# Reading the moving operand by two runs in turn in the features, gates, branches, values and up projection

## The chip, the cores and the metric

The kernel runs on one core of a Trainium2 chip (trn2). The metric is the device time of one execution in microseconds. Everything is fp32 data; the matmuls take fp32r operands, and a product is made of three matmuls on split operands (high part and low part).

## The reference, cut to what matters

```python
proj = x @ w_in                      # 256 x 1024 @ 1024 x 3528: q, k, v of three mixers, indexer
o_A  = sparse attention, top-64 keys by an indexer;  o_B = dilated windows;  o_C = causal block
gates  = sigmoid(x @ w_gate)         # 3 gates of 1024 channels
merged = sum_b gates_b * (o_b @ w_br_b)
x = LN(alpha * x + merged @ w_out)
h = square(relu(x @ w_up)) @ w_down  # 1024 -> 4096 -> 1024
x = LN(alpha * x + h + sigmoid(x @ w_ple_gate) * (p @ w_ple))
```

256 tokens, width 1024, one layer.

## The kernel before

A weight arrives by DMA in the tile `raw` (five buffers) and is split by `Weights._split`: ScalarE (ACT) casts it to `whi` (L112, L110), VectorE (DVE) and in part GpSimd (POOL) write the rest `wlo` = raw - whi (L119, L123). `W.get` keeps the splits up to four units ahead of use. `prod` (L189) makes one product: the terms hi*hi, hi*lo and lo*hi, in an order that a table `TURN` gives for each 128-row block. The tables `LOW` and `UP` set at which element of their tiles the 128-column blocks of `whi` and `wlo` lie.

The program goes through these stages, in this order on TensorE (PE):

- **First products** (L501): the four query blocks of the indexer, while x and their weights still arrive.
- **Features, values, gates, branches** (up to about 200 us of the span). The stationary operand (lhsT) is a 128x128 weight block, the moving operand is 256 tokens of `xh` or `xl` (x transposed, 8 blocks of 256 tokens one after the other in a partition), the output a `mm` bank in PSUM. `feat` makes one block of 128 features (24 matmuls of 256 columns), `fill("g")` one block of gates (24), `fill("c")` one block of branches B and C (15, the moving operand is `op`), `merge` two blocks of branch A (18) and then the gated sum. `values` has the tokens stationary and the weights moving, 384 or 328 columns. The attention of 16 heads is strung between: `logits` (L356), softmax on DVE and ACT, transposes (L397), product with V (L401, L402). The gates are the work that PE does while a head waits for DVE and ACT.
- **Out projection, first norm, PLE gate** (about 200 to 245 us): the tokens are stationary, 512 columns of weights move.
- **Up projection** (245 to 336 us): 32 blocks `f`. Each has 8 matmuls of 512 columns (L901, the high and the low part of both token blocks at once) and 8 of 256 (L903). `relu2` (L885 to L887) adds the two parts on DVE and squares on ACT.
- **Down projection, second norm** (336 us to the end): tokens stationary, 512 columns of weights move. Pairs of blocks use Strassen's scheme; `load` and `form` (L854 to L865) bring and combine weights for it, in the tiles `xr`, `rows` and `Y`. The tile of `xr` is the one in which `x1`, the input of the up projection, was.

Three engines read a product out of PSUM: ACT in `q_pair` (L294), `k_pair` (L307) and for the gates (L320), DVE in `q_pair` (L295), `k_pair` (L308), the branches (L335, L336), the merge (L671) and `relu2`. The `mm` banks are three.

The out, PLE and down projections already read their moving operand "by two runs in turn": `wide` takes 512 (or 256) columns as two runs of half the length, of which one element of the first and one of the second are read alternately; `pairs` writes the result side by side, and the host has the weights in such an order (`turns`) that the result comes out in natural order. The runs lie 256 elements, 1 KB, apart. All other matmuls read one run after the other; in the text "plain".

The order of the instructions is set by a scheduler at build time, with some order pinned by hand.

Of the kernel before, what the change touches and what calls it, by code (L numbers as in the profile page):

```python
# [11 lines left out]
F32 = mybir.dt.float32  # L12
F32R = mybir.dt.float32r
ALU = mybir.AluOpType
AF = mybir.ActivationFunctionType
# [6 lines left out]
KT = D // 128  # L22
# [121 lines left out]
def hybrid_layer(ctx: ExitStack, tc: tile.TileContext, x0, xn, pT, wqk, wva, wvb, wg, wbc, wba,  # L144
# [39 lines left out]
    def prod(ps, a, b, first, last, hold=False, more=False, low=2):  # L184

        terms = [(0, 0), (0, 1)]
        terms.insert(low, (1, 0))
        for n, (x, y) in enumerate(terms):
            i = pe.matmul(ps, lhsT=a[x], rhs=b[y], start=first and n == 0, stop=last and n == 2,  # L189
                          skip_group_check=more)  # L190
            if hold and n == 0:
                pin(i)
# [7 lines left out]
    def pairs(ps):  # L200
        return ps.rearrange("p (c a) -> p c a", a=2)

    def gemm(ps, units, xs, k=0):

        for u in units:
            hi, lo = W.get(u)
            for o in range(0, hi.shape[1], 128):
                prod(ps, (hi[:, o:o + 128], lo[:, o:o + 128]), xs[k], k == 0, k == len(xs) - 1,
                     low=TURN["g"][k])
                k += 1  # L210

# [6 lines left out]

    xh = p1.tile([128, KT, S], F32R, name="xh")
    xl = p1.tile([128, KT, S], F32R, name="xl")  # L220
    xs = [(xh[:, k], xl[:, k]) for k in range(KT)]
    n_u = [0]

    def add(*a, at=(0, 0), by=DV):
# [51 lines left out]
    def mmbank(shape):  # L276
        t = mm.tile([128, 512], F32, name="mm", tag="mm")
        return t[:, 0:256] if shape == 256 else t
# [5 lines left out]
    def freed(*ins):  # L284


        if banks_first[0]:
            W.after = tuple(i.ins for i in ins)
        return ins[0].ins

    def q_pair(ps, scale=-0.125):

        q = qpool.tile([128, 2, S], F32R, name="q", tag="q")
        i = (act.mul(q[:, 0], ps, scale),  # L294
             dve.scalar_tensor_tensor(q[:, 1], ps, scale, q[:, 0].bitcast(F32), op0=ALU.mult,  # L295
                                      op1=ALU.subtract))
        freed(*i)
        last[:] = (x.ins for x in i)
        return q

    def k_pair(a, b=None):


        k = (kp if b is None else k1).tile([128, 2, S], F32R, name="k", tag="k")
        for d, ps in ((slice(0, 128), a),) if b is None else ((slice(0, 64), a),
                                                             (slice(64, 128), b)):
            freed(act.copy(k[d, 0], ps),  # L307
                  dve.tensor_tensor(k[d, 1], ps, k[d, 0].bitcast(F32), op=ALU.subtract))  # L308
        return k

    n_g, n_c = [0], [0]
# [1 line left out]
    def fill(what):  # L313


        for w in what:
            if w == "g":
                ps = mmbank(256)
                gemm(ps, u_g[n_g[0]], xs)
                freed(act.activation(G[:, n_g[0]], ps, AF.Tanh, scale=0.5))  # L320
                n_g[0] += 1
                continue
            f = n_c[0]
            n_c[0] += 1
            hi, lo = W.get(u_bc[f][0])
            ps = mmbank(512).rearrange("p (i s) -> p i s", i=2)
            for i, (k0, k1) in enumerate(((3, 5), (5, 8))):
                for k in range(k0, k1):
                    c = slice((k - 3) * 128, (k - 2) * 128)
                    prod(ps[:, i], (hi[:, c], lo[:, c]), (op[:, k, 0], op[:, k, 1]), k == k0,  # L330
                         k == k1 - 1, low=TURN["c"][k - 3])
            g = G[:, 3 * f + 1:3 * f + 3]

            for i, o in ((1, ps[:, 1]), (0, g[:, 0])):
                dve.scalar_tensor_tensor(o, g[:, i], 1.0, ps[:, i], op0=ALU.add, op1=ALU.mult)  # L335
            freed(dve.tensor_tensor(g[:, 0], g[:, 0], ps[:, 1], op=ALU.add))  # L336

    def feat(f):
        ps = mmbank(256)
# [27 lines left out]
    def values(units, n, h0, heads, withiw):  # L367
        pss = [mmbank(512) for _ in range(2)]
        for i in range(4):
            hi, lo = W.get(units[i])  # L370
            for j in range(2):
                k = 2 * i + j
                c = slice(j * n, (j + 1) * n)
                for b in range(2):
                    t = slice(b * 128, (b + 1) * 128)
                    prod(pss[b][:, :n], (xh[:, k, t], xl[:, k, t]), (hi[:, c], lo[:, c]),
                         k == 0, k == KT - 1)
        v_out(pss, n, h0, heads, withiw)

# [97 lines left out]
    with ExitStack() as begin:  # L477
        st = begin.enter_context(tc.tile_pool(name="st", bufs=1, side="right"))
        sh = st.tile([128, KT, FIRST * 128], F32R, name="sh")
        st.tile([128, 32], F32, name="gap")  # L480
        sl = st.tile([128, KT, FIRST * 128], F32R, name="sl")
        st.tile([128, 16], F32, name="pad")
        g0 = G.rearrange("p i s -> p (i s)").rearrange("p (k c) -> p k c", k=KT)
        cut = [((0, 384), (384, 768)) if k == 0 else ((0, 768),) for k in range(KT)]
        with tc.high_priority(offset=1000):
            for k in range(KT):
                for i, (a, b) in enumerate(cut[k]):
                    e = nc.scalar if i else nc.sync
                    e.dma_start(g0[:, k, a:b], x0[k, :, a:b])
            for k in range(KT):  # L490
                act.copy(xh[:, k], g0[:, k, 0:S])
                for a, b in cut[k]:
                    a = max(a, S)
                    act.copy(sh[:, k, a - S:b - S], g0[:, k, a:b])
                dve.tensor_tensor(xl[:, k], g0[:, k, 0:S], xh[:, k].bitcast(F32), op=ALU.subtract)
                dve.tensor_tensor(sl[:, k], g0[:, k, S:], sh[:, k].bitcast(F32), op=ALU.subtract)
        first = [next(ps_s if f < 3 else ps_t)[:, 0:S] for f in range(FIRST)]
        for k in range(KT):
            for i, (w, x) in enumerate(((sh, xh), (sh, xl), (sl, xh))):
                for f in range(FIRST):  # L500
                    pe.matmul(first[f], lhsT=w[:, k, 128 * f:128 * f + 128], rhs=x[:, k],  # L501
                              start=k == i == 0, stop=k == KT - 1 and i == 2)
        iq = [q_pair(ps, 0.125) for ps in first]
    tp, wk, wk2, sm = (right(n, b) for n, b in (("tp", 3), ("wk", 3), ("wk2", 2), ("sm", 6)))
# [156 lines left out]
    def merge(p):  # L661
        hi, lo = W.get(u_ba[p][0])
        ps = mmbank(512).rearrange("p (f s) -> p f s", f=2)
        for f in range(2):
            for k in range(3):
                c = slice((3 * f + k) * 128, (3 * f + k + 1) * 128)
                prod(ps[:, f], (hi[:, c], lo[:, c]), (op[:, k, 0], op[:, k, 1]), k == 0, k == 2,
                     low=TURN["a"][3 * f + k])
        g6 = G[:, 6 * p:6 * p + 6].rearrange("p (f i) s -> p f i s", f=2)
        g = g6[:, :, 0]  # L670
        dve.scalar_tensor_tensor(g, g, 1.0, ps, op0=ALU.add, op1=ALU.mult)  # L671
        dve.tensor_tensor(g, g, g6[:, :, 1], op=ALU.add)
        for f in range(2):
            o = 8192 + 512 * (2 * p + f)
            m = store[:, o:o + 512].rearrange("p (a s) -> p a s", a=2)
            act.mul(m[:, 0], g[:, f], 0.5)
            dve.scalar_tensor_tensor(m[:, 1], g[:, f], 0.5, m[:, 0].bitcast(F32), op0=ALU.mult,
                                     op1=ALU.subtract)
            mt.append(m)
# [202 lines left out]
            u_dn[k] = [add(wdn[k], 1024)]  # L882

    def relu2(dst, ps):
        dve.tensor_reduce(dst, ps.rearrange("p b a t -> p b t a"), axis=AX.X, op=ALU.add)  # L885
        act.activation(dst, dst, AF.Relu)
        act.activation(dst, dst, AF.Square)  # L887

# [2 lines left out]
    for f in range(32):  # L891
        if f == 16:
            with tc.issue_after(W.loads[-1]):
                load(0)
            with tc.issue_after(W.subs[-1]):
                form(0)
        ps = mmbank(512).rearrange("p (b a t) -> p b a t", b=2, a=2)
        hi, lo = W.get(u_up[f][0])
        cs = [slice(k * 128, (k + 1) * 128) for k in range(KT)]
        for k, c in enumerate(cs):  # L900
            pe.matmul(ps, lhsT=hi[:, c], rhs=x1[:, :, k], start=k == 0, stop=False)  # L901
        for k, c in enumerate(cs):
            pe.matmul(ps[:, :, 0], lhsT=lo[:, c], rhs=x1[:, :, k, 0], start=False,  # L903
                      stop=k == KT - 1)
        if f not in half_of:
            spare = f % 2 == 0
            q = (p3.tile([128, 2, 128], F32, name="q1", tag="q1") if spare else
# [166 lines left out]
def _layout(x, p, w_in, w_gate, w_br_a, w_br_b, w_br_c, w_out, ln1_g, ln1_b, w_up, w_down,  # L1074
# [14 lines left out]
    va = np.concatenate([ar(AV, 64), ar(BV, 256), ar(IW, 8)])  # L1089
    vb = ar(CV, 384)  # L1090

    def moving(w, j):
        n = w.shape[1]
        kt = w.shape[0] // 128
        return w.reshape(kt // j, j, 128, n).transpose(0, 2, 1, 3).reshape(kt // j, 128, j * n)

    def turns(w):
        return w.reshape(w.shape[0], 2, 256, 2).transpose(0, 1, 3, 2).reshape(w.shape)

    gate = np.concatenate([ar(b * D + f * 128, 128) for f in range(8) for b in range(3)])  # L1100
    br = np.concatenate([w_br_a[0], w_br_b[0], w_br_c[0]], axis=0)
# [40 lines left out]
```

## Time and profile before

| | |
|---|---|
| median of 3 runs | 425.36 us (424.82 to 425.51) |
| profiled execution | 426.09 us, its span 424.3 us |
| clock granted to TensorE | 0.997 |
| PE, weight loads (PEld), DVE, ACT, POOL busy | 97%, 89%, 83%, 66%, 28% of the span |
| DMA | 84.30 MB, mean 199 GB/s |

A line such as L189 stands for all products, so its groups are told apart by the names of the tiles (`mm<-xh,whi`: written tile, then what is read) and by shape. Matmuls overlap in the pipeline: the duration of one in a row is from its start to its modelled end, and is longer than the distance to the next. The distance, here called the period, is read in the chain of waits, where an unbroken stretch has a length and a count.

### The profile page before, as it was taken

Reading aid. Unit: us, or ns where it says so; the run is one execution under the profiler, and the core shown is the slowest. Engines: PE = TensorE matmul, PEld = TensorE weight load, DVE = VectorE, ACT = ScalarE, POOL = GpSimd, SP = SyncE. Lnnn points to the kernel's source line nnn. Section 1 sums busy time; section 2 is a strip of 40 time slices with the busy share of each in tenths; the row PEclk is TensorE's granted clock in tenths of the full one; section 3 lists DMA queues with packets and bytes.
Section 4 is the critical chain, followed back from the end, with each engine's and each line's share of the span. In section 5 each row is a group of like instructions: output and inputs, shape, how many; then the busy total and the mean of one; then the engine's idle time right before and its main releaser. Section 6 shows DMA issues by size and latency. Waiting matters only on the chain.

```text
span 424.3 us, 7821 instructions
## 1 busy us (share of the span) xinstructions
PE 412.9 (97%) x2804; PEld 378.2 (89%) x2804; DVE 351.7 (83%) x646; ACT 278.7 (66%) x530; POOL 119.1 (28%) x128
## 2 busy tenths in 40 slices
PE   7999999999999999999999999999999999999993
PEld 7989999999999999999887888888888888788883
DVE  4969668977777679879977889989998789899856
ACT  5868366396797785866705568887888756567320
POOL 1568455264353558500000002332320000000001
PEclk9999999999999999999999999999999999999998
DMA  8795976468474407479780686786675177555602
GB/s 291 282 320 157 250 250 204 147 206 273 127 227 137 131 0 269 141 221 336 253 297 13 227 277 199 228 284 173 192 213 182 62 289 242 160 188 188 211 2 100
DMA packets 28300, 84.30 MB, mean 199 GB/s; under 512 B 2992, under 2 KB 7128, under 8 KB 27876
## 3 DMA queue, kind: packets, MB, share of 16 engines
q1 hardware_dynamic: 26880, 79.41, 57.7%
q10 hardware_dynamic: 1284, 4.32, 3.1%
q8 instruction: 22, 0.36, 0.4%
q14 instruction: 18, 0.15, 0.1%
q0 software_dynamic: 96, 0.06, 0.0%
HBM read 81.88 MB, written 1.90 MB: 197 GB/s over the span
## 4 chain that ended last, share of the span: by engine, by line
PE 72%; DVE 10%; DMA 4%; ACT 2%; issue 2%; SPq 0%; DVEq 0%; ACTq 0%
PE mm L189 33%; PE mm L901 14%; PE b L189 13%; PE mm L903 7%; DVE wlo L119 6%; DMA xr<-in_wdn_dram 3%; PE b L356 2%; DMA raw<-in_wdn_dram 1%; PE b L397 1%; ACT whi L112 1%; DVE Y L863 1%; PE b L401 1%; DVE xr L864 1%; DVE rows L863 1%; ACT ri L526 1%
## 5 line engine op out<-in xcount | busy, mean ns | idle before, releaser
L112 ACT CAST whi<-raw 128x1024 fp32r<-128x1024 f32 (+3 forms) x92 | 89.7, 987 | 37.4 <-PE b L189 12.8
L123 DVE TENSOR_TENSOR wlo<-raw,whi 128x256 fp32r<-128x256 f32 (+3 forms) x118 | 96.8, 844 | 16.7 <-ACT whi L112 14.4
L189 PE MATMUL mm<-xh,whi 128*128 128x256 f32 x336 | 90.3, 280 | 0.0
L189 PE MATMUL mm<-xl,whi 128*128 128x256 f32 x336 | 88.1, 279 | 0.0
L123 POOL TENSOR_TENSOR wlo<-raw,whi 128x384 fp32r<-128x384 f32 (+1 forms) x50 | 68.4, 1378 | 70.3 <-ACT whi L112 69.7
L189 PE MATMUL mm<-xh,wlo 128*128 128x256 f32 x336 | 80.8, 282 | 0.3 <-DVE k L308 0.3
L189 PEld LDWEIGHTS mm<-xh,whi 128*128 128x128 f32 x336 | 63.2, 188 | 0.8
L901 PE MATMUL mm<-x,whi 128*128 128x512 f32 x256 | 63.4, 390 | 0.0
L189 PEld LDWEIGHTS mm<-xl,whi 128*128 128x128 f32 x336 | 63.2, 188 | 0.1
L189 PEld LDWEIGHTS mm<-xh,wlo 128*128 128x128 f32 x336 | 58.0, 188 | 0.9 <-DVE k L308 0.5
L189 PE MATMUL b<-whi,store 128*128 128x512 f32 x168 | 52.7, 381 | 0.3 <-DVE b L974 0.3
L901 PEld LDWEIGHTS mm<-x,whi 128*128 128x128 f32 x256 | 45.8, 188 | 7.5
L119 DVE TENSOR_TENSOR wlo<-raw,whi 128x1024 fp32r<-128x1024 f32 (+2 forms) x38 | 43.0, 1154 | 3.0 <-ACT whi L112 3.0
L718 POOL TENSOR_TENSOR rs<-rs,half 128x1 f32<-128x1 f32 x4 | 2.7, 664 | 145.1 <-DVE rs L717 145.1
L110 ACT CAST whi<-raw 128x256 fp32r<-128x256 f32 x64 | 36.7, 617 | 10.0 <-PE mm L901 5.9
L189 PEld LDWEIGHTS b<-whi,store 128*128 128x128 f32 x168 | 31.7, 189 | 5.2 <-DVE b L974 0.7
L903 PEld LDWEIGHTS mm<-x,wlo 128*128 128x128 f32 x256 | 33.8, 188 | 2.5
L903 PE MATMUL mm<-x,wlo 128*128 128x256 f32 x256 | 34.3, 277 | 0.0
L189 PE MATMUL b<-wlo,store 128*128 128x512 f32 x84 | 32.2, 384 | 0.7 <-DVE wlo L119 0.6
L924 POOL TENSOR_TENSOR a<-a 128x128 f32<-128x128 f32 x7 | 6.3, 899 | 60.4 <-ACT a L887 48.9
L189 PE MATMUL mm<-op,whi 128*128 128x256 f32 x128 | 22.5, 280 | 0.0
L189 PE MATMUL b<-whi,x 128*128 128x512 f32 x64 | 19.8, 384 | 0.1
(223 smaller groups left out, 823.3 us busy)
## 6 DMA issues: line engine op xcount, KB each, us to landing
raw<-in_wup_dram SPq DMA_DIRECT2D x32, 512.0 KB
raw<-in_wg_dram SPq DMA_DIRECT2D x24, 512.0 KB
raw<-in_wqk_dram SPq DMA_DIRECT2D x18, 512.0 KB
raw<-in_wdn_dram SPq DMA_DIRECT2D x18, 512.0 KB
raw<-in_wout_dram SPq DMA_DIRECT2D x8, 512.0 KB
raw<-in_wpg_dram SPq DMA_DIRECT2D x8, 512.0 KB
T<-tabd SPq DMA_DIRECT2D x24, 128.0 KB
xr<-in_wdn_dram SPq DMA_DIRECT2D x6, 512.0 KB
```

Of the source, the lines that this page charges most:

```text
L110: i = nc.scalar.copy(blocks(hi, a, b), blocks(r, a, b))
L112: i = nc.scalar.copy(hi, r)
L119: i = e.tensor_tensor(lo[:, x], r[:, x], hi[:, x].bitcast(F32), op=ALU.subtract)
L123: i = e.tensor_tensor(blocks(lo, *x), blocks(r, *x), blocks(hi, *x).bitcast(F32), op=ALU.subtract)
L189: i = pe.matmul(ps, lhsT=a[x], rhs=b[y], start=first and n == 0, stop=last and n == 2, skip_group_check=more)
L356: m = pe.matmul(ss[2 * n + h][:, QC[b]], lhsT=q[d, x, c], rhs=k[d, y, 0:128 * (b + 1)], start=i == 0, stop=i == 2)
L397: pe.transpose(t[:, 128 * i:128 * i + 128], P[:, 128 * i:128 * i + 128], ident)
L401: pe.matmul(v, lhsT=V[:, 0, vh], rhs=pt[:, :, 0:256], start=True, stop=False)
L863: dve.tensor_tensor(t[:, 0:1024], r[:, 512:1536], r[:, 0:1024], op=ALU.subtract)
L901: pe.matmul(ps, lhsT=hi[:, c], rhs=x1[:, :, k], start=k == 0, stop=False)
L903: pe.matmul(ps[:, :, 0], lhsT=lo[:, c], rhs=x1[:, :, k, 0], start=False, stop=k == KT - 1)
L924: pool.tensor_tensor(sums[2], a11, a21, op=ALU.subtract)
```

## The change

It makes the matmuls of L501, of features, gates, branches A, B, C, of the values and of the up projection read their moving operand by two runs in turn. For `xh`, `xl` and `op` the runs are the two halves of 256 tokens, 128 elements (512 B) apart. For the values they are the halves of 384 or 328 weight columns (768 or 656 B), and the host orders these columns for it (`turns` in `moving`), so the result is in natural order. For `x1` in the up projection they are the two token blocks, 2048 elements (8 KB) apart. Every output is written contiguously into its bank as before. Where tokens move, token c and token c+128 now lie side by side in PSUM, and whoever reads the bank (`order`) reads it with a step of two elements; the tile it writes (`halves`) keeps its order. `relu2` reads the two parts 256 elements apart in place of 128, and the tokens with a step of two. The gated product in `merge` becomes two instructions of 256 in place of one of 512. The tables `TURN`, `LOW` and `UP` stay.

```diff
+    def inturn(t):
+        return t.rearrange("p (a c) -> p c a", a=2)
+    def order(ps):
+        return ps.rearrange("p (c a) -> p a c", a=2)
+    def halves(t):
+        return t.rearrange("p (a c) -> p a c", a=2)
...
-                prod(ps, (hi[:, o:o + 128], lo[:, o:o + 128]), xs[k], k == 0, k == len(xs) - 1,
+                prod(pairs(ps), (hi[:, o:o + 128], lo[:, o:o + 128]), xs[k], k == 0, k == len(xs) - 1,
...
-    xs = [(xh[:, k], xl[:, k]) for k in range(KT)]
+    xs = [(inturn(xh[:, k]), inturn(xl[:, k])) for k in range(KT)]
...
-        i = (act.mul(q[:, 0], ps, scale),
-             dve.scalar_tensor_tensor(q[:, 1], ps, scale, q[:, 0].bitcast(F32), op0=ALU.mult,
+        hi, lo, ps = halves(q[:, 0]), halves(q[:, 1]), order(ps)
+        i = (act.mul(hi, ps, scale),
+             dve.scalar_tensor_tensor(lo, ps, scale, hi.bitcast(F32), op0=ALU.mult,
...
-                freed(act.activation(G[:, n_g[0]], ps, AF.Tanh, scale=0.5))
+                freed(act.activation(halves(G[:, n_g[0]]), order(ps), AF.Tanh, scale=0.5))
...
-                    prod(pss[b][:, :n], (xh[:, k, t], xl[:, k, t]), (hi[:, c], lo[:, c]),
+                    prod(pairs(pss[b][:, :n]), (xh[:, k, t], xl[:, k, t]),
+                         (inturn(hi[:, c]), inturn(lo[:, c])),
...
-        dve.scalar_tensor_tensor(g, g, 1.0, ps, op0=ALU.add, op1=ALU.mult)
+        for f in range(2):
+            o = halves(g[:, f])
+            dve.scalar_tensor_tensor(o, o, 1.0, order(ps[:, f]), op0=ALU.add, op1=ALU.mult)
...
-        dve.tensor_reduce(dst, ps.rearrange("p b a t -> p b t a"), axis=AX.X, op=ALU.add)
+        dve.tensor_reduce(dst, ps.rearrange("p a t b -> p b t a"), axis=AX.X, op=ALU.add)
...
-            pe.matmul(ps, lhsT=hi[:, c], rhs=x1[:, :, k], start=k == 0, stop=False)
+            pe.matmul(ps, lhsT=hi[:, c], rhs=x1[:, :, k].rearrange("p b a t -> p a t b"),
+                      start=k == 0, stop=False)
...
-            pe.matmul(ps[:, :, 0], lhsT=lo[:, c], rhs=x1[:, :, k, 0], start=False,
-                      stop=k == KT - 1)
+            pe.matmul(ps[:, 0], lhsT=lo[:, c], rhs=x1[:, :, k, 0].rearrange("p b t -> p t b"),
+                      start=False, stop=k == KT - 1)
```

The same is done with `k_pair`, the branches in `fill` and `merge`, and L501.

On no engine does an instruction change its place; what differs is shapes, and the pairs in `merge`. On DVE, where the merges end and the out projection is about to begin (L671 is the gated product, L672 the sum, L677 the low part of the merged features that the out projection loads as weights), the rows before are:

```order
L671 SCALAR_TENSOR_TENSOR G<-G,mm 128x2x256
L336 TENSOR_TENSOR G<-G,mm 128x256
L119 TENSOR_TENSOR wlo<-raw,whi 128x1024
L672 TENSOR_TENSOR G<-G 128x2x256
L671 SCALAR_TENSOR_TENSOR G<-G,mm 128x2x256
L119 TENSOR_TENSOR wlo<-raw,whi 128x1024
L671 SCALAR_TENSOR_TENSOR G<-G,mm 128x2x256
L677 SCALAR_TENSOR_TENSOR store<-G,store 128x256
```

In the changed kernel, where L688, L689 and L694 are the same three lines, the same place on DVE reads:

```order
L688 SCALAR_TENSOR_TENSOR G<-G,mm 128x256 x2
L348 TENSOR_TENSOR G<-G,mm 128x256
L119 TENSOR_TENSOR wlo<-raw,whi 128x1024
L689 TENSOR_TENSOR G<-G 128x2x256
L688 SCALAR_TENSOR_TENSOR G<-G,mm 128x256 x2
L119 TENSOR_TENSOR wlo<-raw,whi 128x1024
L688 SCALAR_TENSOR_TENSOR G<-G,mm 128x256 x2
L694 SCALAR_TENSOR_TENSOR store<-G,store 128x256
```

Three instructions more stand ahead of the first low part that the out projection needs, and nothing else moved.

More of the change, by code (lines that the diff above doesn't have):

```diff
@@ L306, in k_pair @@
                                                              (slice(64, 128), b)):
-            freed(act.copy(k[d, 0], ps),
-                  dve.tensor_tensor(k[d, 1], ps, k[d, 0].bitcast(F32), op=ALU.subtract))
+            hi, lo, ps = halves(k[d, 0]), halves(k[d, 1]), order(ps)
+            freed(act.copy(hi, ps), dve.tensor_tensor(lo, ps, hi.bitcast(F32), op=ALU.subtract))
         return k
@@ L329, in fill @@
                     c = slice((k - 3) * 128, (k - 2) * 128)
-                    prod(ps[:, i], (hi[:, c], lo[:, c]), (op[:, k, 0], op[:, k, 1]), k == k0,
+                    prod(pairs(ps[:, i]), (hi[:, c], lo[:, c]),
+                         (inturn(op[:, k, 0]), inturn(op[:, k, 1])), k == k0,
                          k == k1 - 1, low=TURN["c"][k - 3])
             g = G[:, 3 * f + 1:3 * f + 3]
-            for i, o in ((1, ps[:, 1]), (0, g[:, 0])):
-                dve.scalar_tensor_tensor(o, g[:, i], 1.0, ps[:, i], op0=ALU.add, op1=ALU.mult)
-            freed(dve.tensor_tensor(g[:, 0], g[:, 0], ps[:, 1], op=ALU.add))
+            g, ps = ([halves(g[:, i]) for i in range(2)], [order(ps[:, i]) for i in range(2)])
+            for i, o in ((1, ps[1]), (0, g[0])):
+                dve.scalar_tensor_tensor(o, g[i], 1.0, ps[i], op0=ALU.add, op1=ALU.mult)
+            freed(dve.tensor_tensor(g[0], g[0], ps[1], op=ALU.add))
     def feat(f):
@@ L500, in hybrid_layer @@
                 for f in range(FIRST):
-                    pe.matmul(first[f], lhsT=w[:, k, 128 * f:128 * f + 128], rhs=x[:, k],
+                    pe.matmul(pairs(first[f]), lhsT=w[:, k, 128 * f:128 * f + 128],
+                              rhs=inturn(x[:, k]),
                               start=k == i == 0, stop=k == KT - 1 and i == 2)
@@ L666, in merge @@
                 c = slice((3 * f + k) * 128, (3 * f + k + 1) * 128)
-                prod(ps[:, f], (hi[:, c], lo[:, c]), (op[:, k, 0], op[:, k, 1]), k == 0, k == 2,
+                prod(pairs(ps[:, f]), (hi[:, c], lo[:, c]),
+                     (inturn(op[:, k, 0]), inturn(op[:, k, 1])), k == 0, k == 2,
                      low=TURN["a"][3 * f + k])
@@ L896, in hybrid_layer @@
                 form(0)
-        ps = mmbank(512).rearrange("p (b a t) -> p b a t", b=2, a=2)
+        ps = mmbank(512).rearrange("p (a t b) -> p a t b", a=2, b=2)
         hi, lo = W.get(u_up[f][0])
@@ L1090, in _layout, with turns @@
     vb = ar(CV, 384)
+    def turns(w, n=512):
+        m = len(w)
+        return w.reshape(m, -1, n // 2, 2).transpose(0, 1, 3, 2).reshape(m, -1)
     def moving(w, j):
         n = w.shape[1]
+        w = turns(w, n)
         kt = w.shape[0] // 128
         return w.reshape(kt // j, j, 128, n).transpose(0, 2, 1, 3).reshape(kt // j, 128, j * n)
-    def turns(w):
-        return w.reshape(w.shape[0], 2, 256, 2).transpose(0, 1, 3, 2).reshape(w.shape)
     gate = np.concatenate([ar(b * D + f * 128, 128) for f in range(8) for b in range(3)])
```

## The prediction

> **What bounds the kernel now.** I read the engines' busy times first, then the 20 us stretches, the chain of waits, and the groups with their shapes kept apart. The busy times, and four of the stretches (columns: PE, PEld, DVE, ACT, POOL busy, granted clock, share of DMA, GB/s):
>
> ```profile
> PE 412.9 (97%) x2804; PEld 378.2 (89%) x2804; DVE 351.7 (83%) x646; ACT 278.7 (66%) x530; POOL 119.1 (28%) x128
> ...
> 100.00:120.00 20.00, 20.00 (x180) 19.29 (x179) 15.62 (x43) 15.96 (x34) 9.80 (x7) 1.00 0.57 177
> 180.00:200.00 20.00, 20.00 (x173) 19.90 (x172) 17.58 (x32) 12.95 (x21) 0.74 (x1) 1.00 0.85 276
> 300.00:320.00 20.00, 20.00 (x121) 17.74 (x120) 19.56 (x30) 17.08 (x37) 5.77 (x8) 1.00 0.66 204
> 380.00:400.00 20.00, 19.64 (x91) 16.59 (x90) 19.96 (x23) 11.77 (x13) 0.00 (x0) 1.00 0.60 206
> ```
>
> PE is the bound up to the end of the up projection, at full clock. DVE is close behind it at 300 us and has taken over at 380 us. So what counts for the change is the period of PE's matmuls, and whether DVE lets PE go faster. The periods stand in the chain of waits (start, length, what): plain matmuls of 256 columns (features and gates, at the end branches) in the first three rows, then the 512s and the 256s of one block of the up projection, then 512s and 256s of the down projection, which are already read by two runs in turn.
>
> ```profile
> 40.24 7.58 PE mm L189 x64
> 105.90 7.50 PE mm L189 x64
> 184.93 14.70 PE mm L189 x129
> ...
> 262.51 1.81 PE mm L901 x8
> 264.33 0.91 PE mm L903 x8
> ...
> 408.58 5.18 PE b L189 x24
> 413.76 3.58 PE mm L189 x32
> ```
>
> Length by count is the period: 118, 117 and 114 ns for the plain 256s (a missing record inflates the first two); I take 115. An up block has 226 ns per 512 and 114 per 256. In turn it is 215.8 ns per 512 (5.18/24) and 111.9 per 256 (3.58/32). A second witness is the mean duration, kept apart by shape:
>
> ```profile
> L189 PE MATMUL mm<-xh,whi 128*128 128x256 f32 x336 | 90.3, 280 | 0.0
> L189 PE MATMUL mm<-xl,whi 128*128 128x256 f32 x336 | 88.1, 279 | 0.0
> L901 PE MATMUL mm<-x,whi 128*128 128x512 f32 x256 | 63.4, 390 | 0.0
> L903 PE MATMUL mm<-x,wlo 128*128 128x256 f32 x256 | 34.3, 277 | 0.0
> L189 PE MATMUL mm<-op,whi 128*128 128x256 f32 x128 | 22.5, 280 | 0.0
> L189 PE MATMUL mm<-op,wlo 128*128 128x256 f32 x64 | 15.3, 279 | 0.3 <-DVE wlo L123 0.3
> L189 PE MATMUL mm<-whi,xh 128*128 128x384 f32 x16 | 5.4, 335 | 0.0
> L189 PE MATMUL mm<-whi,xh 128*128 128x328 f32 x16 | 5.1, 320 | 0.0
> L189 PE MATMUL b<-whi,PL 128*128 128x512 f32 x8 | 2.7, 380 | 0.0
> L189 PE MATMUL mm<-whi,store 128*128 128x256 f32 x16 | 3.1, 275 | 0.0
> ```
>
> In turn (last two rows) a 512 is 10 ns shorter and a 256 2 to 5 ns shorter than plain.
>
> **What the change costs and brings, step by step.**
>
> *Features and gates*: 42 blocks of 24 matmuls, 1008 (three groups of 336), 115 - 111.9 = 3.1 ns each: 3.1 us. Ends: 2.1 ns (by the row at 184.93) gives 2.1 us, 5 ns (by the durations) 5.0 us. *Branches*: 128 + 64 = 192 at 2 ns: 0.4 us. *Values*: a 384 in turn should last, between 275 and 380, 328 ns, so 7 ns less, and a 328 305, so 15 less; 48 of each (one row of three terms shown): 1.1 us. *Up*: 256 x (226 - 215.8) = 2.6 us and 256 x (114 - 111.9) = 0.5 us. *L501* waits for x to arrive; nothing. Sum on PE: 7.7 us.
>
> [...]
>
> *PSUM read with a step of two*. No row has step two. The nearest reads stand here, DVE first: the up projection's reduction takes its 512 values with a step of 128, a plain sum takes 512 in order.
>
> ```profile
> L885 DVE TENSOR_REDUCE a<-mm 128x256 f32<-128x512 f32 x23 | 15.6, 684 | 2.8 <-PE mm L903 2.7
> L974 DVE TENSOR_TENSOR b<-b,Y 128x512 f32<-128x512 f32 x2 | 1.4, 690 | 0.0
> L671 DVE SCALAR_TENSOR_TENSOR G<-G,mm 128x512 f32<-128x512 f32 x4 | 2.7, 681 | 0.0
> L335 DVE SCALAR_TENSOR_TENSOR mm<-G,mm 128x256 f32<-128x256 f32 x8 | 3.3, 416 | 0.0
> L320 ACT ACTIVATE G<-mm 128x256 f32<-128x256 f32 x24 | 9.1, 380 | 3.7 <-PE mm L189 3.5
> L774 ACT ACTIVATE PL<-mm 128x512 f32<-128x512 f32 x4 | 2.4, 597 | 11.8 <-PE mm L189 11.8
> ```
>
> DVE pays nothing for a step (684 against 690), so nothing for step two. For ACT there is no stepped PSUM read; the lower end is 0, the upper one a doubled streaming time, which is 597 - 380 = 217 ns per 256 values. I take 0, by DVE's rows, and keep 217 ns x about 49 reads (24 gates, 16 q, 9 k) = 10.6 us of ACT time as a rival.
>
> *Merge*: one 512 becomes two 256s, 2 x 416 - 681 = 151 ns, four times, three of them ahead of the first low part that the out projection loads. That place is tight. DVE's last pause before it ends at 189.24, DVE writes that part at 199.03, and PE loads it as weights at 199.68:
>
> ```profile
> 189.24 0.96 DVE L123 TENSOR_TENSOR wlo<-raw,whi 128x768 fp32r<-128x768 f32 x1 [1.19 <-ACT whi L112]
> ...
> 199.03 0.42 DVE L677 SCALAR_TENSOR_TENSOR store<-G,store 128x256 fp32r<-128x256 f32 x1
> ...
> 199.68 0.19 PEld L189 LDWEIGHTS b<-whi,store 128*128 128x128 f32 x1
> ```
>
> 0.23 us to spare. Without a pause in front of it the part comes 0.45 us later, while PE comes some 0.2 us sooner (about 100 matmuls of 114 ns in that stretch, 2 ns each). PE waits 0.45 + 0.2 - 0.23, some 0.4 us; with what DVE's next parts add I charge 0.5.
>
> *Heads*. PE's order is fixed; between a head's logits and its transposes stand some 10 us of gate matmuls, and they shrink by 2.7%, so 0.3 us, while the softmax on DVE and ACT doesn't. Where nothing is to spare, that comes back as a wait. Two such places, ACT's last scaling and the first transpose that needs it:
>
> ```profile
> 91.43 0.79 ACT L417 ACTIVATE eb<-eb,r 128x128 f32<-128x128 f32 x2
> ...
> 92.30 0.27 PE L397 MATMUL b<-ident,eb 128*128 128x128 f32 x1
> ...
> 112.79 0.80 ACT L417 ACTIVATE e<-e,r 128x128 f32<-128x128 f32 x2
> ...
> 113.24 0.33 PE L397 MATMUL b<-ident,e 128*128 128x128 f32 x1
> ```
>
> Less than 0.1 us to spare in both. I found about eight places among the 16 heads under 0.5 us; at 0.15 us each the loss is 1.2 us. Ends: 0 and 2.4 (all eight, in full).
>
> *Up*: DVE is busy 19.56 of 20 us in the stretch at 300, so a block's 2.72 us (1.81 + 0.91) holds 2.66 of DVE's work, and PE alone would take 8 x 215.8 + 8 x 111.9 = 2.62. PE had no idle time there, so the splits are ahead of it and can lend some; I charge 0.2.
>
> *Down* starts with transfers into the tile that the up projection has just read out, and then runs through DVE:
>
> ```profile
> 335.05 0.92 PE mm L903 x8
> 336.37 0.43 SPq L856
> 336.83 4.83 DMA xr<-in_wdn_dram
> ```
>
> It moves forward as a whole by what is gained before it and gets no shorter.
>
> Sum: 7.7 - 0.5 - 1.2 - 0.2 = 5.8 us. The profiled execution takes 426.09 us (its span of 424.3 and 1.8 around it), which leaves 420.3; it stands 0.7 above the median of 425.36, so I predict 419.5 for the median.
>
> **Rivals.**
>
> *Reading in turn loses at the new distances.* Every row in turn has its runs 1 KB apart; here they are 512 B, 656, 768 B and 8 KB apart. The weight blocks stay where the tables put them. If a 256 at 512 B goes to the 118 ns of the worst plain stretch, 3 ns x 1200 = 3.6 us are lost in front in place of 3.5 gained; with the up projection's 3.1 and the losses of 1.9 that is 425.4 + 3.6 - 1.1 - 3.1 + 1.9, about 427. It decides from about 2 ns per 256 on, if the up projection still gains (3.1 + 1.1 - 1.9 = 2.3 us over 1200). If 8 KB fails as well, it is 430. For it: no row has these distances. Against: two stationary tiles (`PL`, `store`) and two lengths gain alike. Chance 0.14. [...]
>
> *The 256s stay at 114 to 115.* Two loads of weights and a matmul may simply not go faster; in-turn 256s come from 32 matmuls alone. Then features, gates, branches and 256s of the up projection bring nothing, 3.7 us with the values and the 512s remain, and the losses fall to about 0.9: 422.6. Chance 0.11.
>
> *DVE holds the up projection.* If DVE's 2.66 us is the block's time, 32 x 0.04 = 1.3 us are lost, at worst all of 3.1: 421 to 422.5. Against it: DVE's splits were never late (PE has no idle time there). Chance 0.10.
>
> *ACT pays for step two.* Each head's q, and each gate between, is 0.2 us later in ACT's queue, so the eight tight places lose 0.4 more each: 419.5 + 3.2 = 422.7. Chance 0.08. [...]
>
> *Nothing to measure*: two of these together, 424.6 to 425.4. Chance 0.07.
>
> **How the numbers follow.** 0.50 for the forecast (own range 417 to 422), 0.11, 0.10 and 0.08 for the three that leave part of the gain, 0.07 for no change, 0.14 for the slower one. What a measurement here can tell from no change is 0.2%, 0.85 us. Faster 0.79, same 0.07, slower 0.14. The low end is the durations' 5 ns in front (419.5 - 1.9 - 1.2 without head losses = 416.4); the high end, 424.5, takes in the partial gains.
>
> **What would show it.** In the changed kernel's chain, unbroken 256s of gates at about 112 ns and eight 512s of the up projection in 1.73 us in place of 1.81; the gates' ACTIVATE still near 380 and the reduction near 684 ns; a wait of half a microsecond of PE at the start of the out projection; small new waits at L397, L401 or L356; from the first xr transfer to the end 87.5 us as before (424.3 - 336.8). The prediction is wrong if the 256s come out above 115 ns, if ACT's reads near 600, or if the down projection grows by what was gained before it.

## The result, and the profile after

The changed kernel takes 420.25 us (median of 4 runs, 419.57 to 420.44), the kernel before beside it 425.44 (424.82 to 425.86): a ratio of 0.9876, with a 95% interval of 0.9859 to 0.9894. The profiled execution took 420.38 us, its span is 418.6 us.

The busy times, and two of the stretches (PE, PEld, DVE, ACT, POOL busy, granted clock, share of DMA, GB/s):

```profile
PE 405.4 (97%) x2804; PEld 373.6 (89%) x2804; DVE 350.7 (84%) x650; ACT 277.4 (66%) x530; POOL 120.5 (29%) x128
...
180.00:200.00 20.00, 20.00 (x166) 19.56 (x165) 18.00 (x33) 12.61 (x19) 0.00 (x0) 1.00 0.81 280
300.00:320.00 20.00, 20.00 (x125) 18.39 (x124) 19.76 (x33) 17.95 (x40) 5.39 (x7) 1.00 0.70 204
```

The granted clock is full in both kernels (0.997 and 0.996), so a shorter period is not a faster clock. PE's busy time fell by 412.9 - 405.4 = 7.5 us, the span by 5.7: PE now idles 13.2 us in place of 11.4. These 1.8 us are what the waits have to account for.

The chain of waits (start, length, what), with an unbroken row of gates and one block of the up projection:

```profile
45.38 9.20 DMA raw<-in_wqk_dram
...
104.70 7.34 PE mm L189 x64
...
125.16 3.57 PE mm L189 x32
...
185.24 8.70 DMA raw<-in_wout_dram
...
262.55 1.73 PE mm L918 x8
...
264.27 0.89 PE mm L921 x8
...
331.55 4.58 DMA xr<-in_wdn_dram
```

3.57/32 is 111.6 ns for a 256, 1.73/8 is 216 for a 512, 0.89/8 is 111 for the up projection's 256s. Ahead of the down projection the chain of before has no transfer; this one has four, x at 1.65, gate weights at 39.81 and the two shown. PE hardly stops for them (the waits below), so they tell what now ends its waits, not how much time is lost. Of the one at 185.24, out weights, there is more below. By shape (busy us, mean ns):

```profile
L189 PE MATMUL mm<-xh,whi 128*128 128x256 f32 x336 | 89.2, 278 | 0.0
L918 PE MATMUL mm<-x,whi 128*128 128x512 f32 x256 | 60.7, 379 | 0.0
L921 PE MATMUL mm<-x,wlo 128*128 128x256 f32 x256 | 33.7, 275 | 0.0
L902 DVE TENSOR_REDUCE a<-mm 128x256 f32<-128x512 f32 x23 | 15.6, 680 | 0.6 <-PE mm L921 0.3
L330 ACT ACTIVATE G<-mm 128x256 f32<-128x256 f32 x24 | 9.1, 380 | 2.7 <-PE mm L189 2.5
L189 PE MATMUL mm<-whi,xh 128*128 128x384 f32 x16 | 5.2, 326 | 0.0
L189 PE MATMUL mm<-whi,xh 128*128 128x328 f32 x16 | 4.9, 309 | 0.0
```

The matmuls are shorter by 2 to 11 ns than in the prediction's rows. PSUM with a step of two costs ACT nothing (L330, 380 ns before and after) and DVE nothing (L902, 680 against 684). PE's waits, summed by who ended them (us, times, longest), first of the kernel before, then of the changed one:

```profile
PE b L501 <- ACT sh L494: 1.0, 1, 1.0
...
PE mm L189 <- DVE k L308: 0.3, 1, 0.3
```

```profile
PE mm L189 <- DVE k L318: 0.8, 1, 0.8
PE b L514 <- ACT sh L507: 0.7, 1, 0.7
PE b L189 <- DVE store L694: 0.7, 1, 0.7
...
PE mm L189 <- DVE V L399: 0.6, 1, 0.6
```

L318 (L308 before), L399 and L694 are 0.5, 0.6 and 0.7 us of new waiting; L501, now L514, gives 0.2 back (0.75 us after 0.96).

### The profile page after: what moved, and what is told of

It reads as the page before. It is cut to its first block, busy times and chain, and to the rows that moved or that the text cites. A ratio compares the mean times of both kernels' runs of the same rounds, so it can differ in the third digit from the quotient of the medians.

```text
span 418.6 us, 7824 instructions
## 1 busy us (share of the span) xinstructions
PE 405.4 (97%) x2804; PEld 373.6 (89%) x2804; DVE 350.7 (84%) x650; ACT 277.4 (66%) x530; POOL 120.5 (29%) x128
## 4 chain that ended last, share of the span: by engine, by line
PE 66%; DVE 15%; DMA 10%; issue 4%; ACT 2%; POOL 1%; SPq 1%; DVEq 0%; ACTq 0%; POOLq 0%
PE mm L189 26%; PE mm L918 13%; PE b L189 12%; PE mm L921 7%; DVE wlo L119 6%; PE b L368 2%; DMA xr<-in_wdn_dram 2%; DMA raw<-in_wqk_dram 2%; DMA raw<-in_wout_dram 2%; PE b L514 2%; DVE wlo L123 2%; DMA G<-in_x_dram 1%; ACT whi L112 1%; PE b L410 1%; DMA raw<-in_wg_dram 1%
## 5 line engine op out<-in xcount | busy, mean ns | idle before, releaser
L189 PE MATMUL mm<-xh,whi 128*128 128x256 f32 x336 | 89.2, 278 | 0.0
L189 PE MATMUL mm<-xl,whi 128*128 128x256 f32 x336 | 86.9, 276 | 0.0
L189 PE MATMUL mm<-xh,wlo 128*128 128x256 f32 x336 | 79.9, 279 | 1.3 <-DVE k L318 0.8
L189 PEld LDWEIGHTS mm<-xh,whi 128*128 128x128 f32 x336 | 64.4, 192 | 0.9
L189 PEld LDWEIGHTS mm<-xl,whi 128*128 128x128 f32 x336 | 64.5, 192 | 0.1
L918 PE MATMUL mm<-x,whi 128*128 128x512 f32 x256 | 60.7, 379 | 0.0
L942 POOL TENSOR_TENSOR a<-a 128x128 f32<-128x128 f32 x7 | 7.3, 1044 | 58.4 <-ACT a L904 52.8
```

Source lines behind the costliest of these rows:

```text
L918: pe.matmul(ps, lhsT=hi[:, c], rhs=x1[:, :, k].rearrange("p b a t -> p a t b"), start=k == 0, stop=False)
L942: pool.tensor_tensor(sums[2], a11, a21, op=ALU.subtract)
```

## Experiments

*1 and 2: each half of the change alone.* The up projection's edits on the kernel before:

```diff
-        dve.tensor_reduce(dst, ps.rearrange("p b a t -> p b t a"), axis=AX.X, op=ALU.add)
+        dve.tensor_reduce(dst, ps.rearrange("p a t b -> p b t a"), axis=AX.X, op=ALU.add)
...
-            pe.matmul(ps, lhsT=hi[:, c], rhs=x1[:, :, k], start=k == 0, stop=False)
+            pe.matmul(ps, lhsT=hi[:, c], rhs=x1[:, :, k].rearrange("p b a t -> p a t b"),
+                      start=k == 0, stop=False)
```

(and the 256s alike), and the changed kernel with these taken back.

> Only the up projection reads in turn (and its reduction reads PSUM with the new steps); everything ahead of it is the kernel before. Theory (each part's own matmuls give its gain, the parts add up, the rest moves as a whole): 512s of the up projection at 216 ns, its 256s at 111.5, gates stay at 114.5; the up projection 3.2 us shorter than the kernel before, all else unchanged, 425.4 - 3.2 = 422.2 us. Rival (DVE holds the up projection, and the whole change only got its full gain there because PE came sooner): up projection shorter by 2 us or less, total above 423.2.

> Features, gates, branches, values and first products read in turn, the up projection reads plain as before. Theory: 256s at 111.6 ns in place of 114.5, values 9 to 11 ns shorter, some 4.4 us of PE time less up to the out projection, of which about 2.4 us come back as waits (bank releases behind DVE's splits, one head or two, one low part at the out projection); the up projection starts 2.0 us sooner than in the kernel before and 423.4 us in all. Rival (the waits come from elsewhere, so the front's gain is smaller or larger than 2.0): below 422.6 or above 424.4.

All ratios here are to the kernel before. Up alone: 422.38 us, ratio 0.9925 [0.9901, 0.9949]. Front alone: 423.60, ratio 0.9959 [0.9944, 0.9974]. 3.1 and 1.9 us by the medians, together 5.0 beside the 5.2 of both. In the chain of up alone the gates are plain and the up blocks short; in front alone it is the other way round:

```profile
106.06 7.50 PE mm L189 x64
...
293.66 1.73 PE mm L901 x8
```

```profile
104.57 7.34 PE mm L189 x64
...
294.07 1.81 PE mm L918 x8
```

With up alone, DVE is at 19.77 us of 20 in the stretch at 300 and PE at 20.00, so PE's whole gain there arrives. The theory holds for both.

*3 and 4: where the weights lie.* The tables `LOW`, `UP` and `TURN` taken out of the kernel before and of the changed one: every weight block stands right behind the one before, and all blocks use one order of terms.

```diff
-    UP = (16, *range(192, 1088, 128)), (64, *range(208, 1104, 128))
+    UP = (0, 0)
...
-            u.append([add(w[len(u)], n, at=(40, LOW[t]) if t in LOW else (0, 0),
+            u.append([add(w[len(u)], n, at=(0, 0),
...
-    TURN = {"g": (0, 2, 1, 2, 2, 0, 1, 2), "c": (2, 0, 2, 1, 2), "a": (2, 1, 2, 2, 2, 0)}
+    TURN = {"g": (2,) * 8, "c": (2,) * 5, "a": (2,) * 6}
```

> The kernel before with the tables made flat: every block of weights lies right behind the one before it, from element 0 of its tile, and the three terms come in one order throughout. Theory (plain reads meet the weight load that runs beside them, and how often depends on where the weights lie): periods of plain 256s rise from 114.5 to 116 to 120, of the 512s of the up projection from 227 to 228 to 233; 2 to 7 us slower than the kernel before, 427 to 432 us. Rival (places don't matter, plain is slow by itself): 114.5 and 227 stay, 425.4 less up to 1 us since a split in the up projection is one instruction in place of two.

> The changed kernel with the same flat tables. Theory (in turn, moving read and weight load fall into step, so the place of the weights doesn't matter): 111.6 and 216 ns stay, total within 1 us of the changed kernel, 419.3 to 420.5. Rival (in turn depends on places as plain does, the tables happen to fit): 256s above 114, 512s above 220, total 423 or more.

The kernel before becomes slower: 431.01 us, ratio 1.0131 [1.0107, 1.0155]. The changed kernel does not: 419.60, 0.9874 [0.9842, 0.9906]. Chains, the plain one first:

```profile
106.40 7.76 PE mm L189 x64
...
273.60 1.84 PE mm L901 x8
275.44 0.95 PE mm L903 x8
```

```profile
105.25 7.34 PE mm L189 x64
```

Plain, the up block goes from 1.81 + 0.91 us to 1.84 + 0.95; between the starts of neighbouring matmuls in the trace a plain 256 in front takes 118.2 ns in the mean in place of 114.5. In turn it is 111.6 and 216.1, as with the tables. So plain reads depend here on where the weights lie (in the up projection on that alone, since `TURN` does not act there; in front on the places or the order of terms, which were changed together), and reads in turn do not. The theory's periods are borne out; its cause, plain reads that meet the weight load beside them and reads in turn that fall into step with it, is my guess, and no run here shows it.

*5 to 8: what "in turn" has to be.* The tokens by four runs of 64; the gates' tokens by two runs but two neighbours of each at a time; the gates' tokens by two runs only 64 values apart, within each half; the up projection's 512s by four runs of 128.

```diff
+    def many(t):
+        return t.rearrange("p (a c) -> p c a", a=4)
...
+    def by_twos(t):
+        return t.rearrange("p (a c e) -> p c a e", a=2, e=2)
...
+    def near(t):
+        return t.rearrange("p (b a c) -> p b c a", b=2, a=2)
...
-            pe.matmul(ps, lhsT=hi[:, c], rhs=x1[:, :, k].rearrange("p b a t -> p a t b"),
+            pe.matmul(ps, lhsT=hi[:, c], rhs=x1[:, :, k].rearrange("p b a t -> p t a b"),
```

The first three are in the first three kernels, in the place of `inturn`; the last line is the fourth kernel's.

> The changed kernel, but where tokens move (features, gates, branches, first products) 256 tokens are read by four runs of 64 in turn, and PSUM is read with a step of four; values and up projection stay at two runs. Theory (with two runs each run is read at the pace at which the weight load reads its block, so that the two, once in step, don't meet again; with four runs the pace is half of that and they meet now and then): 256s of gates at 112.5 to 118, spread over several ns, total 1 to 5 us above the changed kernel, 421 to 425. Rival (any order in which neighbours in time aren't neighbours in memory does): 111.6 with no spread, 420.2 as the changed kernel. In both the gates' ACTIVATE stays at 380 ns if a step in PSUM costs ACT nothing.

> The changed kernel, but the gates read two neighbouring tokens of the first run, then two of the second, and so on, so every 8 bytes of PSUM are again read together; everything else stays. Theory (pace): the average pace of each run is as with one token at a time, so 111.6 ns, at most 112.5, total 420.2. Rival (what helps is that no two accesses in a row lie side by side): 113 to 114.5 for the 576 matmuls of the gates, features stay at 111.6, total up to 1.6 us above, 421.8.

> The changed kernel, but the gates alone read the tokens by two runs that lie 64 values (256 B) apart, in turn within each half of 128, in place of 128 values (512 B) apart; features stay as they are. ACT puts the values back. Theory one (the number of runs in turn is what counts: two are good at any distance seen): gates stay at 111.6 ns per 256, the time near 420. Theory two (256 B apart is too near, which made the kernel with four runs of 64 slow, 140 ns): gates at 130 to 150 ns, 432 to 445 us.

> The changed kernel, but the up projection's 512s read four runs of 128 in turn, all of them 512 B or more apart, in place of two; their 256s read two runs as before, and write every second place of PSUM. Theory one (number of runs): 512s longer by as much per value as with four runs of 64 tokens (140 against 111.6 per 256), so about 270 ns in place of 216, 256 x 54 ns = 13.8 us more, about 434 us, less what DVE hides. Theory two (distance): 512s at 216 ns, the time near 420.

Four runs of tokens: 451.84 us, 1.0625 [1.0595, 1.0654]. Two neighbours at a time: 449.24, 1.0564 [1.0537, 1.0591]. Two runs 256 B apart: 419.72 (one run), nothing lost. Up by four: 437.24 (one run). What was expected of the first two, by theory and by rival, was far off: neither had expected a 256 above 118 ns, so both are refuted as they stood. Starts of neighbouring matmuls of the timeline, four runs of tokens and then two neighbours at a time:

```profile
119.74 0.30 PE L189 MATMUL mm<-xh,whi 128*128 128x256 f32 x1
...
120.30 0.31 PE L189 MATMUL mm<-xl,whi 128*128 128x256 f32 x1
```

```profile
115.73 0.33 PE L189 MATMUL mm<-xl,whi 128*128 128x256 f32 x1
...
116.91 0.34 PE L189 MATMUL mm<-xh,wlo 128*128 128x256 f32 x1
```

Four steps in 0.56 us are 140 ns, seven in 1.18 us 169 ns, against 111.6. The chains of the other two, 256 B apart and up by four:

```profile
104.75 7.34 PE mm L189 x64
```

```profile
252.03 0.89 PE mm L921 x8
252.92 2.26 PE mm L918 x8
```

Two runs are good at 256 B as at the other distances (7.34 us, as in the changed kernel's stretch at 104.70). Four runs are bad at 64 values as at 512 B and more: 2.26/8 = 282 ns per 512 is 0.55 ns per value, and 140/256 is 0.55 too. So with one value at a time the number of runs decides here, not the distance; theory one of the last two kernels holds (up by four came to 437 where 434 was expected). Why four runs, or pairs out of two, lose is open.

Whether neighbours in memory are read one right after the other does not order them either: of the reads that never do so, those by two runs are the fastest (111.6) and those by four are slow (140); plain reads, which always do, take 114.5 to 118.2, and the reads that take two neighbours at a time are the slowest (169).

ACT's read of the gates with a step of four took 381 ns in the four-run kernel, so for ACT this step costs nothing either (380 with a step of two and in order):

```profile
L336 ACT ACTIVATE G<-mm 128x256 f32<-128x256 f32 x24 | 9.1, 381 | 16.2 <-PE mm L189 16.1
```

*9 and 10: the wait at the out projection.* First without the extra instructions in the merge: branch A is left plain, so that one 512 reads the bank again. Then the changed kernel with the load of X (1 MB), which ACT issues at 185.57 in the midst of the loads of out weights, put on SyncE behind the last of them.

```diff
-        for f in range(2):
-            o = halves(g[:, f])
-            dve.scalar_tensor_tensor(o, o, 1.0, order(ps[:, f]), op0=ALU.add, op1=ALU.mult)
+        dve.scalar_tensor_tensor(g, g, 1.0, ps, op0=ALU.add, op1=ALU.mult)
```

```diff
-    act.dma_start(X, xn)
+    with tc.issue_after(W.loads[-1]):
+        nc.sync.dma_start(X, xn)
```

> The changed kernel, but branch A in merge reads plain, so the gated product is one instruction of 512 again. Theory one (the wait for a low part at the out projection comes from the three or four instructions more on DVE ahead of it): the wait of 0.7 us on the low parts falls to 0.3 or less, total 0.2 to 0.4 us below the changed kernel. Theory two (it comes from the out weights, whose transfers don't land sooner just because PE is there sooner, so ACT casts and DVE splits them late and the low part stands in DVE's queue behind three of them): ACT still waits about 2 us or more for the transfer of out weights at 191 us, the wait on the low part stays at 0.5 to 1.7, total within 0.3 us of the changed kernel.

> The changed kernel, but the transfer of x in rows (1 MB, for the first norm) is issued on SyncE behind the last transfer of out weights, not on ACT's queue in the middle of them. Theory two of the wait (transfers of out weights are what is late): they land sooner by about the 3 to 4 us that 1 MB takes at 280 GB/s, ACT's wait for them at 191 us of 2.1 goes to 0.5 or less, PE's wait on the low part to 0.2 or less, total 0.5 to 0.9 us below the changed kernel, 419.5. Theory one (the merge's extra instructions): PE's wait stays at 0.5 or more, total as the changed kernel, 420.2.

Merge plain: 420.97 us, 0.9890 [0.9847, 0.9933]; X later: 419.70, 0.9866 [0.9843, 0.9888]. The totals do not tell them apart. PE's wait for the low part, of merge plain and of X later:

```profile
PE b L189 <- DVE store L691: 1.4, 1, 1.4
```

```profile
PE b L189 <- DVE store L694: 0.4, 1, 0.4
```

In these traces the wait goes with how long ACT sits before its cast of out weights. That row in the changed kernel, with the tables flat, with X later, and, from the experiments above, with up by four:

```profile
194.03 1.06 ACT L112 CAST whi<-raw 128x1024 fp32r<-128x1024 f32 x1 [2.10 <-DMA raw<-in_wout_dram]
```

```profile
195.87 1.06 ACT L112 CAST whi<-raw 128x1024 fp32r<-128x1024 f32 x1 [3.89 <-DMA raw<-in_wout_dram]
```

```profile
192.55 1.05 ACT L112 CAST whi<-raw 128x1024 fp32r<-128x1024 f32 x1 [0.92 <-PE mm L189]
```

```profile
193.01 1.05 ACT L112 CAST whi<-raw 128x1024 fp32r<-128x1024 f32 x1 [0.92 <-PE mm L189]
```

ACT waits 2.10 and 3.89 us in the first two, where the transfer lands late, and 0.92 in the others, where it waits for PE. PE's wait for L694 is 0.7, 1.6, 0.4 and 0.4 us. Up by four leaves the load of X where it was, and so do near runs, with 0.92 and 0.4 too; front alone has 3.19 and 1.6, merge plain 3.02 and 1.4. (The profiled executions of merge plain and of flat tables, 422.38 and 422.28 us, are the longest of their four.) So there are two parts: 0.4 us that stay when no transfer is late, and up to 1.2 that differ from trace to trace.

*The late transfer.* From issue to landing this load of 512 KB takes 4.2 us in both kernels with X later (the other is number 11). With X beside it, it takes 6.9 in near runs and in up by four, 8.7 in the changed kernel, and 9.7 to 10.4 in front alone, flat tables and merge plain. So theory two is supported as to the transfer: the load of X holds it up; at 6.9 us it is still in time, at 8.7 ACT waits for it. Open is why it takes 3.6 to 4.1 us in the three kernels whose front is plain (before, up alone, the first with flat tables), where X is issued 0.5 us behind it; with the front in turn it is issued 0.3 us behind.

*The 0.4 that stay.* DVE's rows from one split to the third low part, first of the kernel before, then of up by four:

```profile
192.56 1.22 DVE L119 TENSOR_TENSOR wlo<-raw,whi 128x1024 fp32r<-128x1024 f32 x1
...
202.63 3.49 DVE L119 TENSOR_TENSOR store<-raw,store 128x1024 fp32r<-128x1024 f32 x3
206.04 0.76 DVE L677 SCALAR_TENSOR_TENSOR store<-G,store 128x256 fp32r<-128x256 f32 x2
```

```profile
190.10 1.22 DVE L119 TENSOR_TENSOR wlo<-raw,whi 128x1024 fp32r<-128x1024 f32 x1
...
203.84 0.75 DVE L694 SCALAR_TENSOR_TENSOR store<-G,store 128x256 fp32r<-128x256 f32 x2
```

DVE has no pause in either. From the first row to the last it takes 13.48 us before and 13.74 with the pairs: 0.26 more, which is what the four pairs of L688 cost. It reaches the split 2.46 us sooner than before, PE the out projection 2.63 us sooner (196.83 for 199.46): another 0.17. Together that is 0.43, the wait; theory two had expected 0.2 or less with X later. So the extra instructions are a part of it, and theory one is not refuted; merge plain saves them, but its trace has a late transfer, and no run shows it without one.

*11: both ideas together.* Flat tables and X later, on the changed kernel.

> The changed kernel with weight blocks contiguous and one order of terms (the tables LOW, UP and TURN flat), and the load of X issued by SyncE behind the last load of out weights. Each alone ran as fast as the changed kernel within its interval (0.9874 and 0.9866 of the kernel before, against 0.9876). Theory: 256s at 111.6, 512s at 216.1, PE's wait for the first low parts of the out projection at most 0.4 us; 419.5 us, between 418.9 and 420.5. Rival: without the tables the late weights come back as a wait of 1.6 us, 421.

419.87 us, 0.9885 [0.9867, 0.9903]: the wait for L694 is 0.4 and the periods stay, so the late weights of the rival do not come, but the time is that of the changed kernel within the intervals. No version tried here beats it. What the run shows is that the tables can go at no measurable cost: ACT's instructions fall from 530 to 498 and DVE's from 650 to 618.

## Why the prediction was right, and where it was not

Forecast for the profiled execution 420.3 us, measured 420.38; for the median 419.5, measured 420.25, inside the range. The 0.7 us that I took off for the median belonged to the one profiled execution of before; the changed kernel's stands only 0.13 above its median.

**Gain on PE.** Said 7.7, measured 7.5. By the starts of neighbouring matmuls: 1008 x (114.5 - 111.65) = 2.9 for features and gates (said 3.1), 192 x (113.9 - 111.6) = 0.4 for the branches (0.4), 48 x 9 and 48 x 11 ns by the durations = 1.0 for the values (1.1; 7 and 15 ns had been said, two errors that cancel), 256 x (226.8 - 216.2) = 2.7 and 256 x (113.4 - 111.3) = 0.5 for up (2.6 and 0.5). The periods of 24 and 32 matmuls elsewhere in the program carried over to 1712 others. Matched one by one in the two traces, PE's steps are 7.9 us shorter, leaving the waits aside.

**Step two.** Taken as nothing for DVE and for ACT; both measured (680 against 684 ns, 380 against 380). DVE's rows were a fair neighbour for ACT, for which there was none.

**Merge: the sum near, its parts not.** The loss was said to be 0.5 us, and 0.74 came. *Place:* the row at 199.68 that I took for the load of the first low part belongs to a high part. The wait came later, at the third block. DVE stands there behind three splits of out weights, in both kernels (at 202.63 before, at 200.60 now):

```profile
199.34 0.74 DVE L688 SCALAR_TENSOR_TENSOR G<-G,mm 128x256 f32<-128x256 f32 x2
200.00 0.69 DVE L689 TENSOR_TENSOR G<-G 128x512 f32<-128x512 f32 x1
200.60 3.49 DVE L119 TENSOR_TENSOR store<-raw,store 128x1024 fp32r<-128x1024 f32 x3
204.01 0.75 DVE L694 SCALAR_TENSOR_TENSOR store<-G,store 128x256 fp32r<-128x256 f32 x2
...
204.48 1.35 PE L189 MATMUL b<-whi,store 128*128 128x512 f32 x5 [0.74 <-DVE store L694]
```

The first matmul of the out projection starts at 199.46 before and at 196.67 after, 2.79 us sooner; the low part at 206.04 and 204.01, 2.03 sooner. The difference, 0.76, is the wait of 0.74. Nothing was to spare there: the matmul that needs this low part already starts 0.36 us after its neighbour before, in place of 0.22. *Size:* two 256s were charged 2 x 416 - 681 = 151 ns; but DVE's instructions overlap here (the pair runs to 200.08, the next starts at 200.00), and from the pair's start to the next start it is 200.00 - 199.34 = 0.66 us, against 0.59 for the single 512 of before (201.44 to 202.03): 0.07. Four pairs ahead of the third block are 0.26 us, where 0.45 was charged for three; PE comes 0.17 sooner, 0.2 said. *Left out:* the other 0.33, from 13.74 us on DVE to 204.01 - 189.94 = 14.07, is the late transfer: it is issued 2.5 us sooner than before (185.24 for 187.73) and lands 2.1 us later (193.93 for 191.83). The prediction asked what DVE had to spare and not what its data waited for, though its row for 180 to 200 us has a DMA share of 0.85.

**Heads.** 1.2 us said for eight tight places. Matmul by matmul, PE stands longer at three heads, by 0.3, 0.2 and 0.1 us, some 0.6 in all; one is the second place named (113.24 before), where the transpose now starts 0.30 us after the matmul ahead of it; before it was 0.12:

```profile
111.77 0.28 PE L189 MATMUL mm<-xh,whi 128*128 128x256 f32 x1
112.07 0.33 PE L410 MATMUL b<-ident,e 128*128 128x128 f32 x1
```

At the first (92.30) no wait appears. Such waits also differ between traces: up alone, whose front is that of the kernel before, has one of 0.48 us at a head (L401) where the kernel before has none. So one trace does not settle this term.

**Banks, a term that the sum had not.** What I had not looked for is the release of `mm` banks: PE stops where DVE, behind a split, is late to read a bank.

```profile
37.70 1.64 DVE L123 TENSOR_TENSOR wlo<-raw,whi 128x640 fp32r<-128x640 f32 x1
39.26 0.41 DVE L318 TENSOR_TENSOR k<-mm,k 128x256 fp32r<-128x256 f32 x1
...
39.82 0.35 PE L189 MATMUL mm<-xh,wlo 128*128 128x256 f32 x1 [0.77 <-DVE k L318]
```

This one was 0.3 us already and became 0.8, the one at V (L399) is new with 0.6. Both stand in every trace of a kernel whose front reads by two runs throughout, with 0.5 to 0.9 and 0.6 us.

**The sum of the losses.** By the starts of PE's matmuls, banks cost 1.2 us more than before, heads 0.6, the out projection 0.8, a late `wlo` ahead of the branches 0.1; the first products give 0.1 back and the down projection 0.4. That is 2.2, and 7.9 - 2.2 is the 5.7 by which the span fell. (PE's idle time grew by 1.8 only, because the modelled end of a matmul covers the first part of a wait: a 256 lasts 278 ns in its row, at a period of 111.6.) Said were 1.9. That these are so near is in part luck: heads came to half of what was charged and up to nothing, and banks, which were not in the sum, filled the place.

**Up.** 0.2 was charged for DVE, nothing was lost: the stage went from 91.6 us (the chain's end at 335.97) to 88.3, 3.25 less, which is PE's whole gain there. DVE at 19.76 of 20 us still kept ahead. **Down** moved as a whole, but for the 0.4 us: 418.6 - 331.55 = 87.05 us from the first transfer of xr to the end, 87.5 said. That transfer itself took 4.58 us in place of 4.83.

**Rivals.** That other distances lose (0.14) is refuted at 512 B and 8 KB by the result and at 256 B by the gates with near runs; that ACT pays (0.08) by L330; that DVE holds up (0.10) by the run of up alone; that the 256s stay (0.11) by the chain; that there is nothing to measure (0.07) by the result.

## What to carry to other kernels

Where PE is busy all the time, read the period from an unbroken row of the chain of waits (length by count) rather than from the duration of one matmul, and compare it with the period of the same shape elsewhere in the program: it carried over here to within 0.4 ns. Then charge the loss to whatever does not move with PE, and follow it two steps back: to the engine's queue ahead of the late instruction, and to the transfer ahead of that. Two instructions for one cost the distance between starts, not the sum of their durations: the pair on DVE 0.07 us here, not 0.15. And before a wait in one trace is put down to a change, look for the same wait in every other trace with the same code there: this one was 0.4 us in some and 1.6 in others.

## What the runs showed that I had not expected

A 256 read plain took 114.5 ns with the weights placed by the tables and 118.2 without; by two runs in turn 111.6 wherever the weights lay. In turn was only good here with two runs and one value at a time: four runs take 140 ns per 256 and 282 per 512, two neighbours of two runs 169 per 256. And a load of 512 KB that takes 4.2 us from issue to landing took 6.9 to 10.4 where a load of 1 MB was issued 0.33 us behind it from another queue; with the second load moved to the end, the total stayed the same within 0.2%.
